# Strassen's method for three of eight pairs of k-tiles in w_up and the gates

## The chip, the cores and the metric

One core of a Trainium2 chip runs the whole program. The metric is the device time of one execution in microseconds (us), lower is better. The engines are TensorE (PE; PEld is its weight load), VectorE (DVE), ScalarE (ACT), GpSimd (POOL) and SyncE (SP, which issues the loads here).

## What is computed

Two layers of an encoder on 256 tokens of width 2048, all in float32:

```
proj  = x @ w_in            -> q/k/v of attention A and B, gate_A, gate_B (2048 columns each)
merged = sigmoid(gate_A) * (A @ w_pa) + sigmoid(gate_B) * (B @ w_pb)
x = LayerNorm(alpha * x + merged @ w_out)
gate, up = split(x @ w_up)                    # w_up: 2048 x 11264
x = LayerNorm(alpha * x + (silu(gate) * up) @ w_down)   # w_down: 5632 x 2048
```

## The kernel before

**Three matmuls for one product.** Each float32 operand is split into a high part (rounded to fp32r by a ScalarE copy) and a low part (VectorE: value minus high part). A product of two k-tiles is high x high + high x low + low x high: three matmuls into the same PSUM bank (`rows_product`, L215 to L217).

**Pieces.** Every weight matrix goes through a list of pieces of 512 KB (128 partitions x 1024 values: two k-tiles of 512 columns, or four of 256). `load_to` issues a piece's load on SP into one of N_RAW raw buffers, `split_to` makes `hi` and `lo` (L128, L129) in two of the N_UNITS unit buffers of 4 KB per partition, and `mm` runs its matmuls. `run` walks the list in order: for piece m it first writes out the splits up to AHEAD_SPLIT pieces further on (more near a LayerNorm), then `pre`, the matmuls, `post`, and then one entry of `background`. Every engine's queue follows this order; semaphores do the rest.

**Products.** `gemm_a` has x as the stationary operand: per k-tile and half of the tokens (t = 0, 1) three matmuls of 512 columns (or 256). One `gemm_a` over 2048 rows of 512 columns is 8 pieces, 96 matmuls, and takes one of the two double banks `acc`. `gemm_w` has the weights stationary (512 and 256 columns alternate). `aux` has four single banks for transposes and attention.

**The stages of a layer.** v, q and k products with attention in the background; the gates (`gate(c)`: two `gemm_a` and sigmoid, c = 0 to 3), each followed by `merge(c)` (w_pa, w_pb, products with the gates, and `turn_block`, which transposes the result); w_out with residual and LayerNorm (`residual_gemm`, `ln_turned`); then for 11 blocks c the gate and up products of w_up, silu (L748), the gating product (L752) and `turn_block`; after blocks 0 to 5 and 6 to 10 `residual_gemm` with that part of w_down. The last 512 columns of a `residual_gemm` with LayerNorm behind it are two blocks of 256 (the second by halves of the tokens).

**Background.** `turn_block` (L402: four transposes for each half, then the split L290, L291), attention, and after each LayerNorm the `affine` steps (L436, L437: res times g plus b; `load_affine` issues the loads into `gb`) are entries of `background`, one taken per piece.

Of the kernel before, what the change touches and what calls it, by code (L numbers as in the profile page):

```python
# [10 lines left out]
F32 = mybir.dt.float32  # L11
# [5 lines left out]
P = 128  # L17
# [20 lines left out]

N_RAW = 6
N_UNITS = 37  # L40
AHEAD_LOAD = 5
AHEAD_SPLIT = 3
AHEAD_NORM = 5
EARLY = 3


# [30 lines left out]
def trunk(ctx: ExitStack, tc: tile.TileContext, x, rel_bias, w_in, sink, w_pa, w_pb, w_out,  # L77
# [28 lines left out]
    background = []  # L106
    state = {"load": 0, "split": 0}
    norms = []

    def piece(src, kk, cc, mm, pre=None, post=None):  # L110
        pieces.append(dict(src=src, kk=kk, cc=cc, mm=mm, pre=pre, post=post))
        return pieces[-1]

    def load_to(m):
        while state["load"] < min(m, len(pieces)):
            pc = pieces[state["load"]]
            pc["raw"] = work.tile([P, pc["kk"], pc["cc"]], F32, name="raw", tag="raw", bufs=N_RAW)
            nc.sync.dma_start(pc["raw"], pc["src"])
            state["load"] += 1

    def split_to(m):
        while state["split"] < min(m, len(pieces)):
            load_to(state["split"] + 1 + AHEAD_LOAD)
            pc = pieces[state["split"]]
            raw = pc["raw"]
            hi = unit([P, pc["kk"], pc["cc"]], F32R, "whi")
            lo = unit([P, pc["kk"], pc["cc"]], F32R, "wlo")
            nc.scalar.activation(hi, raw, AF.Copy)  # L128
            nc.vector.tensor_tensor(out=lo, in0=raw, in1=hi.bitcast(F32), op=ALU.subtract)  # L129
            pc["hi"], pc["lo"] = hi, lo  # L130
            state["split"] += 1
# [118 lines left out]
    def gemm_a_halves(w, k0, k1, c0, width, xs, post, between):  # L250
# [21 lines left out]
        for j in range(k0, k1, kk):  # L272
            src = w[j * P:(j + kk) * P, c0:c0 + width].rearrange("(k p) c -> p k c", p=P)
            piece(src, kk, width, lambda pc, j=j: mm(j, pc))

    def lookup(tiles):
# [118 lines left out]
    def turn_block(src, tiles, name):  # L395

        def half(i):
# [5 lines left out]
            tiles.append(split_unit(ps, name))  # L403
        background.extend([lambda: None, lambda: half(0), lambda: half(1)])

# [243 lines left out]
    def layer(l, xt, pre, turn, after_last):  # L649
# [74 lines left out]
        def merge(c):  # L724
# [31 lines left out]
        after2, between2, ret = after_last(stats2)  # L756
        for half, (c0, c1) in enumerate(((0, 6), (6, 11))):
            for c in range(c0, c1):
                st = {}
                gemm_a(w_up[l], 0, KT, 512 * c, 512, x1s, lambda acc, st=st: post_gate(acc, st),  # L760
                       turn=(turn1 if c == 0 else None))
                gemm_a(w_up[l], 0, KT, D_FF + 512 * c, 512, x1s, lambda acc, st=st: post_up(acc, st))
            residual_gemm(w_down[l], 4 * c0, 4 * c1, lookup(hs), ALPHA if half == 0 else None,
                          None if half == 0 else stats2, after2, between2)
        if l < DEPTH - 1:
# [82 lines left out]
```

## Time and profile before

| what | value |
|---|---|
| median of 3 runs | 2767.43 us (2766.91 to 2768.36) |
| profiled execution | 2767.28 us, span 2765.5 us |
| TensorE busy | 2749.0 us, 99%, 13539 matmuls |
| VectorE busy | 1480.9 us, 54% |
| ScalarE busy | 1168.2 us, 42% |
| DMA | 531.8 MB, mean 192 GB/s |
| mean granted clock of TensorE | 0.998 of 2.4 GHz |

Busy times are sums of durations. Matmuls are pipelined, so a matmul's duration in a row is longer than its share of the time; the distance between the starts of two neighbours is what it costs. For VectorE and ScalarE too a following instruction that waits for nothing starts a little before the former one's end.

### The profile page before, as it was taken

The page shows a single profiled execution, that of the slowest core. Times are in us where ns is not written, and L with a number is a line of the kernel's source. Part 1 is how long each engine was busy: PE and PEld are TensorE (multiplying, and loading weights), DVE is VectorE, ACT ScalarE, POOL GpSimd, SP SyncE. Part 2 cuts the span into 40 slices and gives each one's busy share as a digit, 9 for nine tenths or more (in the row PEclk, how much of TensorE's full clock was granted, in tenths as well). Part 3 has the DMA queues.
Part 4 walks back from the last instruction along what each step waited for, and adds up shares of the span by engine and source line. Part 5 has one row for each costly group of instructions (what it writes and reads, how often), then busy time and mean ns, then how long its engine had stood idle before and what let it go on. Part 6 is the DMA issues. An engine that isn't in the chain of part 4 may idle for free.

```text
span 2765.5 us, 34763 instructions
## 1 busy us (share of the span) xinstructions
PE 2749.0 (99%) x13539; PEld 2319.5 (84%) x13539; DVE 1480.9 (54%) x1688; ACT 1168.2 (42%) x1407; POOL 5.4 (0%) x13
## 2 busy tenths in 40 slices
PE   9999999999999999999999999999999999999998
PEld 7888888888888888888889888888888888888887
DVE  5566554566644544445566655455665444444445
ACT  4454443444333443434344544433544344423441
POOL 0000000000000000000000000000000000000000
PEclk9999999999999999999999999999999999999999
DMA  8866665564655554655656666555645565555554
GB/s 255 241 183 181 185 202 178 187 229 149 225 184 183 208 204 158 211 177 191 215 162 201 179 183 191 177 201 179 232 162 198 183 205 205 183 183 183 187 209 145
DMA packets 359801, 531.84 MB, mean 192 GB/s; under 512 B 52288, under 2 KB 153664, under 8 KB 359636
## 3 DMA queue, kind: packets, MB, share of 16 engines
q1 hardware_dynamic: 358836, 528.31, 58.1%
q8 instruction: 106, 1.74, 0.3%
q10 hardware_dynamic: 800, 1.31, 0.1%
q14 instruction: 59, 0.48, 0.0%
HBM read 522.86 MB, written 6.68 MB: 191 GB/s over the span
## 4 chain that ended last, share of the span: by engine, by line
PE 98%; DVE 1%; DMA 0%; SPq 0%; issue 0%; ACT 0%; DVEq 0%; POOL 0%; ACTq 0%; POOLq 0%
PE acc L217 27%; PE acc L215 27%; PE acc L216 27%; PE acc L202 9%; PE acc L171 5%; PE aux L402 1%; PE aux L297 0%; PE aux L296 0%; PE aux L295 0%; DVE xT L392 0%; PE aux L562 0%; PE aux L528 0%; PE aux L620 0%; PE aux L544 0%; DMA res<-in_x_dram 0%; PE aux L370 0%
## 5 line engine op out<-in xcount | busy, mean ns | idle before, releaser
L129 DVE TENSOR_TENSOR wlo<-raw,whi 128x1024 fp32r<-128x1024 f32 x960 | 1127.4, 1221 | 474.5 <-ACT whi L128 455.4
L128 ACT ACTIVATE whi<-raw 128x1024 fp32r<-128x1024 f32 x960 | 971.5, 1054 | 434.9 <-DMA raw<-in_w_down_dram 142.1
L215 PE MATMUL acc<-whi,xT 128*128 128x512 f32 (+1 forms) x2176 | 848.7, 390 | 0.0
L217 PE MATMUL acc<-whi,xT 128*128 128x512 f32 (+1 forms) x2176 | 842.0, 387 | 0.0
L216 PE MATMUL acc<-wlo,xT 128*128 128x512 f32 (+1 forms) x2176 | 840.8, 386 | 0.0
L217 PEld LDWEIGHTS acc<-whi,xT 128*128 128x128 f32 x2176 | 409.1, 188 | 84.2
L215 PEld LDWEIGHTS acc<-whi,xT 128*128 128x128 f32 x2176 | 409.3, 188 | 80.8 <-issue 0.7
L216 PEld LDWEIGHTS acc<-wlo,xT 128*128 128x128 f32 x2176 | 409.4, 188 | 80.5
L202 PE MATMUL acc<-xT,whi 128*128 128x512 f32 x1088 | 387.0, 399 | 0.0
L171 PE MATMUL acc<-xT,wlo 128*128 128x256 f32 x1088 | 299.6, 280 | 0.0
L215 PE MATMUL acc<-whi,hT 128*128 128x512 f32 (+1 forms) x784 | 288.9, 368 | 0.0
L217 PE MATMUL acc<-whi,hT 128*128 128x512 f32 (+1 forms) x784 | 288.2, 368 | 0.0
L216 PE MATMUL acc<-wlo,hT 128*128 128x512 f32 (+1 forms) x784 | 288.0, 367 | 0.0
L202 PEld LDWEIGHTS acc<-xT,whi 128*128 128x128 f32 x1088 | 203.0, 188 | 43.3
L171 PEld LDWEIGHTS acc<-xT,wlo 128*128 128x128 f32 x1088 | 205.6, 189 | 2.6
L215 PEld LDWEIGHTS acc<-whi,hT 128*128 128x128 f32 x784 | 147.8, 189 | 24.3
L216 PEld LDWEIGHTS acc<-wlo,hT 128*128 128x128 f32 x784 | 147.9, 189 | 24.3
L217 PEld LDWEIGHTS acc<-whi,hT 128*128 128x128 f32 x784 | 147.8, 189 | 24.3
L290 ACT ACTIVATE hT<-aux 128x512 fp32r<-128x512 f32 x44 | 26.3, 598 | 315.2 <-PE aux L402 315.2
L752 DVE TENSOR_TENSOR sg<-sg,acc 128x1024 f32<-128x1024 f32 x22 | 26.9, 1221 | 202.3 <-PE acc L217 202.3
L215 PE MATMUL acc<-whi,mT 128*128 128x512 f32 (+1 forms) x320 | 111.5, 348 | 0.0
L217 PE MATMUL acc<-whi,mT 128*128 128x512 f32 (+1 forms) x320 | 111.0, 347 | 0.0
(133 smaller groups left out, 1503.8 us busy)
## 6 DMA issues: line engine op xcount, KB each, us to landing
raw<-in_w_up_dram SPq DMA_DIRECT2D x352, 512.0 KB, 4.7
raw<-in_w_in_dram SPq DMA_DIRECT2D x320, 512.0 KB, 4.9
raw<-in_w_down_dram SPq DMA_DIRECT2D x176, 512.0 KB, 5.5
raw<-in_w_out_dram SPq DMA_DIRECT2D x64, 512.0 KB, 5.6
raw<-in_w_pb_dram SPq DMA_DIRECT2D x32, 512.0 KB, 5.0
raw<-in_w_pa_dram SPq DMA_DIRECT2D x16, 512.0 KB, 5.9
bias<-ftab SPq DMA_DIRECT2D x96, 64.0 KB, 3.7
ftab<-fb SPq DMA_DIRECT2D x7, 640.0 KB
```

What stands on the lines that cost most here:

```text
L128: nc.scalar.activation(hi, raw, AF.Copy)
L129: nc.vector.tensor_tensor(out=lo, in0=raw, in1=hi.bitcast(F32), op=ALU.subtract)
L171: nc.tensor.matmul(st["acc"][:, n, 0:SEQ], lhsT=lo[:, k, n * P:(n + 1) * P], rhs=xs(4 * j + k)[:, 0, :], start=False, stop=False)
L202: nc.tensor.matmul(acc, lhsT=hi[:, k, n * P:(n + 1) * P], rhs=xs(kt).rearrange("p h t -> p (h t)"), start=first and not turn, stop=last)
L215: nc.tensor.matmul(o, lhsT=xk[:, 0, ts], rhs=hi, start=first, stop=False)
L216: nc.tensor.matmul(o, lhsT=xk[:, 0, ts], rhs=lo, start=False, stop=False)
L217: nc.tensor.matmul(o, lhsT=xk[:, 1, ts], rhs=hi, start=False, stop=last)
L290: nc.scalar.activation(hi, src, AF.Copy)
L402: nc.tensor.transpose(out=ps[:, k, t * P:(t + 1) * P], in_=src[:, t, c0:c0 + P], identity=ident)
L752: nc.vector.tensor_tensor(out=s, in0=s, in1=acc, op=ALU.mult)
```

## The change

`gemm_s` computes a block of 512 columns at c1 and one at c2 (gate_A and gate_B, or gate and up) together. Over a pair of k-tiles, the two token halves, two k-tiles and two column blocks are a 2 x 2 product of blocks; Strassen's form (Winograd's variant, 7 products) needs sums of x blocks, `sum_rows`, made once per layer and stage for the first SUMS = 3 pairs of k-tiles, and sums of weight blocks, made per block. PLAN = "SCSCSCCC": S is a pair of k-tiles with 7 products (four pieces, of which two have a load; VectorE adds t13 and t24 and splits them), C a pair with the usual 8 (two pieces). q1, q5, q6 and q7 take the four aux banks until `fold`, after the third S, brings them into two tiles e and f; q2, q3, q4 and x take both acc tiles, and the last C adds e and f. Pieces before the third S's end are `quiet`: no background is taken there. `turn_block` goes to a list `soon` that is taken before `background`.

It is used for gates c = 1 to 3 and w_up blocks c = 1 to 10, in both layers. w_down's parts follow blocks 0 to 3, 4 to 7 and 8 to 10 (three instead of two). Splits stand five pieces ahead instead of three; there are 7 raw buffers (6 before) and 36 units (37). In C steps 3, 5 and 6 of PLAN the low part of the left piece is made by ScalarE writing -raw and a DMA issued by GpSimd that adds raw to it; this is begun eight pieces ahead (its load eleven).

```diff
-N_RAW = 6
-N_UNITS = 37
+N_RAW = 7
+N_UNITS = 36
+SUMS = 3
+PLAN = "SCSCSCCC"
 AHEAD_LOAD = 5
-AHEAD_SPLIT = 3
+ADDED = (3, 5, 6)
+AHEAD_SPLIT = 5
+AHEAD_ADD = 8
+AHEAD_ADD_LOAD = 11
...
+    def add_to(m):
...
+        while state["add"] < min(m + AHEAD_ADD, len(pieces)):
+            pc = pieces[state["add"]]
+            if pc and pc.get("added"):
+                raw = pc["raw"]
+                pc["hi"], pc["lo"] = unit(list(raw.shape), F32R, "whi"), unit(list(raw.shape), F32R, "wlo")
+                nc.scalar.activation(pc["lo"], raw, AF.Copy, scale=-1.0)
+                nc.gpsimd.dma_start(pc["lo"], raw, accum_op=ALU.add)
+                nc.scalar.activation(pc["hi"], raw, AF.Copy)
+                pc["split"] = lambda pc: None
+            state["add"] += 1
...
+            add_to(m)
             split_to(m + 1 + ahead)
...
-            if background:
-                background.pop(0)()
+            if not pc.get("quiet") and (soon or background):
+                (soon or background).pop(0)()
...
+    def gemm_s(w, c1, c2, xs, sums, post, plan=PLAN):
+        names = {"S": ("q1", "q2", "q3", "q5", "q7", "q6", "q4"),
+                 "C": ("q2", "q2", "q4", "q4", "q3", "q3", "x", "x")}
...
+                st["even"], st["odd"] = acc_tile(), acc_tile()
+                st.update(q2=st["even"][:, 0, :], q3=st["even"][:, 1, :], q4=st["odd"][:, 0, :], x=st["odd"][:, 1, :])
...
+            def split2(pc):
+                raw = b["right"] = pc["raw"]
+                b["t13"] = unit([P, 2, 512], F32, "t13")
+                nc.vector.tensor_tensor(out=b["t13"][:, 0, :], in0=b["left"][:, 0, :], in1=raw[:, 0, :], op=ALU.add)
+                b["b22"] = unit([P, 2, 512], F32R, "b22")
+                split_into(b["b22"][:, 0, :], b["b22"][:, 1, :], raw[:, 1, :])
...
+            def split3(pc):
+                b["t24"] = unit([P, 2, 512], F32, "t24")
+                for o, x0, x1 in ((b["t13"][:, 1, :], b["right"][:, 0, :], b["right"][:, 1, :]),
+                                  (b["t24"][:, 0, :], b["t13"][:, 0, :], b["right"][:, 1, :])):
+                    nc.vector.tensor_tensor(out=o, in0=x0, in1=x1, op=ALU.add)
+                nc.vector.tensor_tensor(out=b["t24"][:, 1, :], in0=b["t24"][:, 0, :], in1=b["left"][:, 1, :], op=ALU.add)
+                b["h13"] = halves(b["t13"])
+            def split4(pc):
+                b["h24"] = halves(b["t24"])
+            def mm1(pc):
+                product("q1", rows(2 * p, 0), pc["hi"][:, 0, :], pc["lo"][:, 0, :])
+                product("q2", rows(2 * p + 1, 0), pc["hi"][:, 1, :], pc["lo"][:, 1, :])
...
+            def mm4(pc):
+                hi, lo = b["h24"]
+                product("q6", total(p, 2), hi[:, 0, :], lo[:, 0, :])
+                product("q4", rows(2 * p + 1, 1), hi[:, 1, :], lo[:, 1, :])
+                if last:
+                    fold()
...
+        def fold():
+            nc.scalar.activation(e[:, 0, :], st["q1"], AF.Copy)
+            nc.vector.tensor_tensor(out=d, in0=e[:, 0, :], in1=st["q6"], op=ALU.subtract)
+            nc.vector.tensor_tensor(out=e[:, 1, :], in0=d, in1=st["q7"], op=ALU.subtract)
+            nc.vector.scalar_tensor_tensor(f[:, 0, :], st["q5"], -1.0, d, op0=ALU.mult, op1=ALU.subtract)
+            nc.vector.scalar_tensor_tensor(f[:, 1, :], st["q5"], -1.0, e[:, 1, :], op0=ALU.mult, op1=ALU.subtract)
...
+            def block(pc, names_, extra):
...
+                for t, n in enumerate(names_):
+                    for k in range(2):
+                        product(n, rows(2 * p + k, t), pc["hi"][:, k, :], pc["lo"][:, k, :])
+                    if last:
+                        nc.vector.tensor_tensor(out=out_[:, t, :], in0=st[n], in1=st[extra][:, t, :], op=ALU.add)
...
         for c in range(4):
-            gate(c)
-            merge(c)
+            if c == 0:
+                gate(c)
+                merge(c)
...
+            else:
+                both(c)
+                merge(c)
...
-        for half, (c0, c1) in enumerate(((0, 6), (6, 11))):
+        chunks = ((0, 4), (4, 8), (8, 11))
+        for part, (c0, c1) in enumerate(chunks):
             for c in range(c0, c1):
                 st = {}
-                gemm_a(w_up[l], 0, KT, 512 * c, 512, x1s, lambda acc, st=st: post_gate(acc, st),
-                       turn=(turn1 if c == 0 else None))
+                if c > 0:
+                    gemm_s(w_up[l], 512 * c, D_FF + 512 * c, x1s, sums, post_both)
+                    continue
```

## Rows read from the trace of the kernel before

**Rows 1.** The page: busy us (share) x instructions, and the chain's shares.

```profile
PE 2749.0 (99%) x13539; PEld 2319.5 (84%) x13539; DVE 1480.9 (54%) x1688; ACT 1168.2 (42%) x1407; POOL 5.4 (0%) x13
...
PE 98%; DVE 1%; DMA 0%; SPq 0%; issue 0%; ACT 0%; DVEq 0%; POOL 0%; ACTq 0%; POOLq 0%
```

**Rows 2.** Timeline of PE in w_up: start us, us, engine, line, operation.

```profile
735.61 0.39 PE L215 MATMUL acc<-whi,xT 128*128 128x512 f32 x1
...
740.83 0.39 PE L217 MATMUL acc<-whi,xT 128*128 128x512 f32 x1
...
741.96 0.39 PE L216 MATMUL acc<-wlo,xT 128*128 128x512 f32 x1
```

**Rows 3.** Timeline of PE in w_out's 256-column block, first and last of 17.

```profile
639.74 0.28 PE L215 MATMUL acc<-whi,mT 128*128 128x256 f32 x1
...
641.66 0.28 PE L216 MATMUL acc<-wlo,mT 128*128 128x256 f32 x1
```

**Rows 4.** Timeline of PE around the transposes of half a block.

```profile
743.54 0.39 PE L217 MATMUL acc<-whi,xT 128*128 128x512 f32 x1
743.78 0.60 PE L402 MATMUL aux<-ident,sg 128*128 128x128 f32 x4
...
744.45 0.40 PE L216 MATMUL acc<-wlo,xT 128*128 128x512 f32 x1
```

**Rows 5.** The gating products of w_up's first part: ns min/median/max, first and last start.

```profile
L752 DVE TENSOR_TENSOR sg<-sg,acc x6: 1220/1220/1222, 696.8 to 919.2; 128x1024 f32<-128x1024 f32 x6
```

**Rows 6.** Window of those five periods: us, busy us (x) of each engine.

```profile
696.80:919.20 222.40, 222.40 (x1001) 184.06 (x1000) 110.88 (x103) 86.00 (x92) 0.00 (x0) 1.00 0.58 197
```

**Rows 7.** Timeline of DVE: neighbours at 692, a read of a product at 741.

```profile
692.08 0.69 DVE L437 TENSOR_TENSOR res<-res,gb 128x512 f32<-128x512 f32 x1
692.69 1.22 DVE L129 TENSOR_TENSOR wlo<-raw,whi 128x1024 fp32r<-128x1024 f32 x1
693.83 0.69 DVE L436 TENSOR_TENSOR res<-res,gb 128x512 f32<-128x512 f32 x1
694.55 0.69 DVE L437 TENSOR_TENSOR res<-res,gb 128x512 f32<-128x512 f32 x1
...
741.25 1.22 DVE L752 TENSOR_TENSOR sg<-sg,acc 128x1024 f32<-128x1024 f32 x1 [9.98 <-PE acc L217]
```

**Rows 8.** Groups of instructions by form: busy us, mean ns, idle before and releaser.

```profile
L129 DVE TENSOR_TENSOR wlo<-raw,whi 128x1024 fp32r<-128x1024 f32 x960 | 1127.4, 1221 | 474.5 <-ACT whi L128 455.4 <-PE acc L216 15.1
L128 ACT ACTIVATE whi<-raw 128x1024 fp32r<-128x1024 f32 x960 | 971.5, 1054 | 434.9 <-DMA raw<-in_w_down_dram 142.1 <-DMA raw<-in_w_up_dram 94.2 <-PE acc L217 66.3
```

**Rows 9.** Waits, SP's and the others': us in total, times, longest us.

```profile
SPq L118 <- DVE wlo L129: 2065.6, 884, 22.4
...
DVE wlo L129 <- ACT whi L128: 455.4, 249, 13.2
...
DVE res L436 <- DMA gb<-in_ln_g_dram: 19.1, 10, 3.3
```

**Rows 10.** DMA: share of 16 engines; issues with KB each and us to landing.

```profile
q1 hardware_dynamic: 358836, 528.31, 58.1%
...
raw<-in_w_up_dram SPq DMA_DIRECT2D x352, 512.0 KB, 4.7
...
gb<-in_ln_b_dram SPq DMA_DIRECT2D x16, 256.0 KB, 6.3
```

**Rows 11.** Timeline of ACT at the start: the seventh xT split.

```profile
27.04 0.59 ACT L290 ACTIVATE xT<-aux 128x512 fp32r<-128x512 f32 x1
```

**Rows 12.** Timeline of PE at the start, with idle time before.

```profile
9.17 0.30 PE L370 MATMUL aux<-ident,res 128*128 128x128 f32 x1 [2.29 <-DMA res<-in_x_dram]
10.46 0.52 PE L370 MATMUL aux<-ident,res 128*128 128x128 f32 x3 [0.98 <-DMA res<-in_x_dram]
...
11.08 0.63 PE L216 MATMUL acc<-wlo,xT 128*128 128x512 f32 x1
...
13.64 0.63 PE L216 MATMUL acc<-wlo,xT 128*128 128x512 f32 x1
```

More of the change, by code (lines that the diff above doesn't have):

```diff
@@ L106, in trunk @@
     background = []
-    state = {"load": 0, "split": 0}
+    soon = []
+    state = {"load": 0, "split": 0, "add": 0, "add_load": 0}
     norms = []
     def piece(src, kk, cc, mm, pre=None, post=None):
-        pieces.append(dict(src=src, kk=kk, cc=cc, mm=mm, pre=pre, post=post))
+        pieces.append(dict(src=src, kk=kk, cc=cc, mm=mm, pre=pre, post=post, split=split_plain))
         return pieces[-1]
@@ L116, in load_to, with split_plain, raw_tile @@
             pc = pieces[state["load"]]
-            pc["raw"] = work.tile([P, pc["kk"], pc["cc"]], F32, name="raw", tag="raw", bufs=N_RAW)
-            nc.sync.dma_start(pc["raw"], pc["src"])
+            if pc["src"] is not None and not pc.get("added"):
+                raw_tile(pc)
             state["load"] += 1
+    def split_plain(pc):
+        raw = pc["raw"]
+        pc["hi"] = unit(list(raw.shape), F32R, "whi")
+        pc["lo"] = unit(list(raw.shape), F32R, "wlo")
+        split_into(pc["hi"], pc["lo"], raw)
+    def raw_tile(pc):
+        pc["raw"] = work.tile([P, pc["kk"], pc["cc"]], F32, name="raw", tag="raw", bufs=N_RAW)
+        nc.sync.dma_start(pc["raw"], pc["src"])
+    def add_to(m):
+        while state["add_load"] < min(m + AHEAD_ADD_LOAD, len(pieces)):
+            pc = pieces[state["add_load"]]
+            if pc and pc.get("added"):
+                raw_tile(pc)
+            state["add_load"] += 1
+        while state["add"] < min(m + AHEAD_ADD, len(pieces)):
+            pc = pieces[state["add"]]
+            if pc and pc.get("added"):
+                raw = pc["raw"]
+                pc["hi"], pc["lo"] = unit(list(raw.shape), F32R, "whi"), unit(list(raw.shape), F32R, "wlo")
[4 more added lines that the diff above has]
+            state["add"] += 1
     def split_to(m):
@@ L124, in split_to @@
             pc = pieces[state["split"]]
[L125 to L130, printed above, removed]
+            pc["split"](pc)
             state["split"] += 1
@@ L403, in half @@
             tiles.append(split_unit(ps, name))
-        background.extend([lambda: None, lambda: half(0), lambda: half(1)])
+        soon.extend([lambda: None, lambda: half(0), lambda: half(1)])
     def ln_scale(stats, t):
@@ L756, in layer, with post_both @@
         after2, between2, ret = after_last(stats2)
-        for half, (c0, c1) in enumerate(((0, 6), (6, 11))):
+        sums = []
+        def post_both(gate_, up_):
+            nc.scalar.activation(gate_, gate_, AF.Silu)
+            nc.vector.tensor_tensor(out=gate_, in0=gate_, in1=up_, op=ALU.mult)
+            turn_block(gate_, hs, "hT")
+        chunks = ((0, 4), (4, 8), (8, 11))
+        for part, (c0, c1) in enumerate(chunks):
             for c in range(c0, c1):
                 st = {}
-                gemm_a(w_up[l], 0, KT, 512 * c, 512, x1s, lambda acc, st=st: post_gate(acc, st),
-                       turn=(turn1 if c == 0 else None))
+                if c > 0:
+                    gemm_s(w_up[l], 512 * c, D_FF + 512 * c, x1s, sums, post_both)
+                    continue
+                gemm_a(w_up[l], 0, KT, 512 * c, 512, x1s, lambda acc, st=st: post_gate(acc, st), turn=turn1)
                 gemm_a(w_up[l], 0, KT, D_FF + 512 * c, 512, x1s, lambda acc, st=st: post_up(acc, st))
-            residual_gemm(w_down[l], 4 * c0, 4 * c1, lookup(hs), ALPHA if half == 0 else None,
-                          None if half == 0 else stats2, after2, between2)
+                pieces[-12]["pre"] = lambda: background.__setitem__(slice(0, 0), [
+                    lambda i=i: sums.append(sum_rows(x1t[i])) for i in range(SUMS)])
+            last = part == len(chunks) - 1
+            residual_gemm(w_down[l], 4 * c0, 4 * c1, lookup(hs), ALPHA if part == 0 else None,
+                          stats2 if last else None, after2, between2)
         if l < DEPTH - 1:
```

87 lines of the change are left out of this document (added).

## The prediction

> **What bounds the kernel now.** I read the page's busy shares and its chain first [rows 1]: TensorE is busy 99% of the span and carries 98% of the chain that ended last, while VectorE is busy 54% and ScalarE 42%. A kernel in that state gets shorter by fewer or cheaper matmuls and by nothing else, as long as the other engines keep up. So the second reading is the price of one matmul. Its duration in the row (0.39 us) is pipelined and overlaps the next one; the price is the distance between starts. From the matmul that starts at 735.61 to the one at 741.96 there are 28 steps, 6.35 us, so 0.2268 us for a 512-column matmul [rows 2]. A 256-column matmul steps by 0.120 us (16 steps in 1.92 us), more than half of that [rows 3]. Turning one half block (four transposes) adds 0.46 us: from 743.54 to 744.45 two matmuls and the transposes take 0.91 us, and two matmuls alone take 0.45 [rows 4]. One pair of w_up products is now 192 x 0.2268 + 2 x 0.46 = 44.5 us, and from the first gating product of a layer to its sixth, five periods, it is 222.4 us, 44.48 each [rows 5], with TensorE busy for all of it [rows 6]. The account of TensorE therefore closes without any hidden idle time.
>
> The third reading is the slack beside it. In that stretch VectorE works 110.9 of 222.4 us and ScalarE 86.0 [rows 6]. VectorE's price is again the distance of starts: 1.14 us for a 1024-wide tensor_tensor, 0.61 us for a 512-wide one, 0.72 us where the next one needs its result [rows 7]. ScalarE's 1024-wide copy lasts 1.05 us [rows 8]. Result to reader is quick: a product's last matmul started at 740.83 and lasts 0.39; VectorE begins to read at 741.25 [rows 2, 7]. Loads run with slack: SP waits 2066 us in all for raw buffers to be freed by the subtraction [rows 9]; a 512 KB load then lands in 4.7 us [rows 10].
>
> **What the change removes.** A Strassen step needs 7 products of 3 matmuls where 8 were: 3 fewer. Three of the eight pairs of k-tiles get it, so 9 fewer of 192 per pair of column blocks. Per layer there are 3 such pairs among the gates and 10 in w_up, two layers: 26. 26 x 9 x 0.2268 = **53.1 us**. The chain carries all of it. The Trainium skill (TensorE: Matmul & The Clock Gate, Back-to-back issue gap) gives N / 2.4 + 2.5, 215.7 ns at 512 columns, by which 50.5 us would go and the result would come out 2.6 us later; the row's 226.8 ns decides.
>
> w_down in three parts instead of two leaves its matmuls as they are but shortens the part that ends in 256-column blocks from 20 to 12 k-tiles: 96 matmuls of 256 become 48 of 512 per layer, 96 x 0.120 - 48 x 0.2268 = 0.6 us, **1.3 us** in two layers. Its four extra updates of res per layer (1.22 us each on VectorE, as its 1024-wide subtraction [rows 8]) lie behind products of 16 us and more.
>
> **What it adds to VectorE and ScalarE.** VectorE, by the steps above: a Strassen pair needs three 1024-wide subtractions and five 512-wide operations, one of them behind its predecessor: 3 x 1.14 + 4 x 0.61 + 0.72 = 6.6 us. TensorE takes 21 x 0.2268 = 4.76 us for it, so **each Strassen pair costs VectorE more than TensorE**. A plain pair costs VectorE 2.28 and TensorE 5.44 us, and where the left low part goes by DMA only 1.14. The whole product: 3 x 6.6 + 7 x 1.14 + fold 2.7 + four adds 2.5 + the gating product 1.2 + two turned halves 1.4 = 35.6 us of VectorE beside 183 x 0.2268 + 0.92 = 42.4 us of TensorE, 84%. ScalarE: 22 copies of 1.05 at the most, six smaller ones of 0.6 [rows 11], silu no longer than a copy: 28 us or less. Neither is the bound on average, so the question is whether VectorE is ever late.
>
> I lay one period out, counted from its first matmul. TensorE: S1 0, C1 4.76, S2 10.2, C2 14.97, S3 20.4, C3 25.2, C4 31.5, C5 37.0, end 42.4 (the two turned halves lie in C3). Splits stand five pieces ahead in VectorE's order. The fold waits for q6 (24.7) and ends at 27.4; then C5's right split 28.5, a turned half (its transposes end at 28.35, ScalarE 0.6) 29.7, next S1's first split 30.8, the second turned half 32.8, S1's second to fourth splits 34.0, 37.1, 38.3. Now VectorE must wait for TensorE at the final adds: q2 39.1, q4 40.5, C1's left split 41.6, q3 42.2, x 43.3, gating product 44.5. The next period's q2 needs the bank freed by the add of q3, at 42.4 + 0.68 = 43.1: 0.9 us to spare. Going on: C1's right split 45.7, S2's four 46.8, 48.0, 51.1, 52.2. S2's third piece is wanted at 54.7: **3.5 us to spare, the smallest lead of a split**. If a split must wait for unit buffers of the piece just finished, S2's third can begin at 3.4 and S3's at 13.6, done by 6.5 and 16.7, wanted at 12.2 and 22.4. So no wait in a plain period.
>
> **Where I do expect waits.** The affine work of res stands in the background list, and background is popped only in pieces that are not quiet: for c = 1, 2, 3 of each layer two affine steps (2 x 1.33 us, from the 0.72 and 0.61 steps) fall between S1's third split and the add of q3. That add then ends at 43.9. The next Strassen product wants the bank at 43.1 (0.8 us late, twice per layer), and the w_down product after c = 3 wants it at 42.4 (1.5 us late): 3.1 per layer, **6.2 us**. If these steps wait for their gb load too (it lands in 6.3 us [rows 10], and affine waited 19.1 us in 10 places [rows 9]) up to 3 us more each, 18 in all; I take none, since in this order SP is waiting for raw buffers freed some 10 us earlier. The other ten places where a Strassen product gives way to a plain one have the bank free within 0.2 us: **2 us**. At the start, up to two more splits go ahead of the sixth to eighth xT split; ScalarE begins the seventh at 27.0 [rows 11], a little over one piece of 2.7 us before its use: between 0 and 2 x 1.14, I take **1.5 us**. The sums of xT (about 2.4 us of VectorE each, twelve) lie beside plain pieces where VectorE has 1.6 us of every 2.7 free, with five splits in hand. Cost nothing; without that cover 29 us.
>
> **The accumulating DMA.** No row shows one, nor a load issued by GpSimd. A plain 512 KB load takes 4.7 us [rows 10]; with two reads and a write for each value I bound it by 4.7 from below and by twice that, 9.4, from above, and take 7. The low part of C2's left half is issued when S1's third piece is done (3.4), after ScalarE's copy 4.5, and is wanted by the second matmul of that piece at 15.2: 10.7 us; C3's has 10.7, C4's 12.7. Inside the bounds it is hidden; the cover is these eight pieces. The Trainium skill (DMA: Bandwidth & Descriptors, Anatomy of one DMA) fits 2.0 us + bytes / 436e3 for a DMA from GpSimd, 3.2 us by estimate, by which the sum stays as it is; no run here shows it. The 78 transfers move 41 MB more beside 528 MB, on engines that are 58% taken now [rows 10].
>
> **Sum.** The profiled execution took 2767.28 us (span 2765.5, 0.15 us under the median of 2767.43): 2767.3 - 53.1 - 1.3 + 6.2 + 2 + 1.5 = 2722.6. VectorE's table has about 20 hand-overs per period that I priced at nothing; a tenth of a microsecond in half the periods brings me to **2724**.
>
> **Rivals.**
> - No wait at all (the table's affine waits vanish because VectorE runs further ahead): 2767.3 - 54.4 = 2713, up to 2719. For it: VectorE is at 84%. 0.18.
> - Forecast, 2719 to 2732. 0.50.
> - VectorE becomes the bound in places: each of 19 subtractions per period stands behind a ScalarE copy of 1.05 us or less, and that wait is VectorE's largest in this trace, 455 us in 249 places [rows 9]. If they cost 0.36 us each, VectorE needs the 42.4 us of TensorE, and 0.4 to 1.3 us of wait per period gives 10 to 34 us: 2732 to 2758. For it: a Strassen pair favours VectorE's lateness by 1.8 us. Against: ScalarE has 14 us free in a period. 0.20.
> - **Slower:** the accumulating DMA lands late. One wait of (landing - 10.7) per period, since the later ones are issued before it. It decides from 12.5 us on: 26 x 1.8 = 47 us eats the gain, the time is then above 2773; at 20 us it is about 2724 + 26 x 9.3 = 2966. A gap also brings the clock down: after idle of 2.29 and 0.98 us matmuls stepped by 0.427 us, the 1.2 GHz level, for 3 us [rows 12]. For it: the operation is unmeasured. Against: 12.5 is 2.7 times a load. The Trainium skill (SBUF — State Buffer, Who interferes with whom) says that GpSimd cannot write descriptors while VectorE runs in a two-port mode, and exempts tensor_tensor from that; VectorE's operations here are tensor_tensor, so by it this rival stays small. 0.09.
> - It doesn't do what it says (matmuls step slower between banks, say by 0.006 us): 2757 to 2773. Against: the plain loop already changes bank every three matmuls at 0.2268. 0.03.
>
> **Numbers.** The likeliest is 2724. From 2710 to 2756 the first three cases are in, all but some 0.13. Faster by over 0.2% (5.5 us, about what a measurement of this kernel tells from no change) 0.88, within 0.03, slower 0.09.
>
> **What will show it.** TensorE: 234 fewer matmuls of 512 columns, steps still 0.227, busy near 2700; period of w_up 42.4 us, longer by about 1 us for c = 1 and 2. VectorE busy for about 1481 + 26 x 16 + 39 = 1940 us (by durations: 4.7 more per Strassen pair, 5.5 for fold and adds, less 3.7 by DMA, then sums and updates). A wait of TensorE for the add of q3 in the first three Strassen products of w_up, none for low parts. GpSimd's DMA landing within 10 us. What would make it wrong: TensorE waiting for `lo` of the added pieces, or for t13 and t24 splits, in every period.

## The result, and the profile after

The changed kernel takes 2731.98 us (median of 4 runs, 2730.58 to 2733.23) beside 2767.17 us for the kernel before (4 runs, 2766.57 to 2768.36): a ratio of 0.9872, 95% interval 0.9855 to 0.9889. It is faster by 35 us, inside the range given and 8 us above the number given; 2731.98 lies at the very edge between the forecast's own band (2719 to 2732) and that of the rival in which VectorE is late in places. The profiled execution took 2733.02 us, with a span of 2731.2 us and a mean granted TensorE clock of 0.997.

The page of after, busy times and DMA: first the lines that answer to [rows 1], then queues and issues as in [rows 10].

```profile
PE 2701.2 (99%) x13209; PEld 2269.0 (83%) x13209; DVE 1894.5 (69%) x2354; ACT 1382.3 (51%) x1679; POOL 72.8 (3%) x91
...
q1 hardware_dynamic: 356788, 528.31, 58.9%
q0 software_dynamic: 11232, 40.90, 8.1%
...
raw<-in_w_up_dram SPq DMA_DIRECT2D x352, 512.0 KB, 5.2
...
wlo<-raw POOLq DMA_DIRECT2D x78, 512.0 KB, 6.9
```

TensorE lost 48 us of busy time and VectorE gained 414, and still TensorE is busy 99% of the span. The new queue q0 holds the 78 accumulating transfers, 41 MB, and lies beside loads that take 59% of the engines. Next, the gating products of w_up in a stretch without other work (name, count, ns min/median/max, first and last start), which answers to [rows 5]:

```profile
L955 DVE TENSOR_TENSOR sg<-sg x3: 1225/1226/1226, 1000.3 to 1085.2; 128x1024 f32<-128x1024 f32 x3
```

Two periods in 84.9 us: 42.45 each, where 44.48 were. What TensorE waits for most in after (what waited and for whom; us in total, times, longest):

```profile
PE aux L549 <- DMA res<-in_x_dram: 2.9, 2, 2.2
PE acc L329 <- DVE sg L414: 2.9, 5, 0.6
PE acc L329 <- DVE sg L908: 2.9, 2, 1.4
PE acc L245 <- DVE sg L414: 1.9, 2, 1.2
PE aux L330 <- DVE tlo L470: 1.6, 2, 0.8
```

L414 is the final add of a Strassen product, L908 the gating product of pa, L470 the low half of a split. Nowhere does TensorE wait for an accumulating DMA.

The chain of waits of after reaches back only into the last LayerNorm, so the account is made from steps: for each pair of neighbouring matmuls, the distance of their starts less the price of that form ([rows 2 to 4]), summed by place.

| term | forecast us | measured us |
|---|---|---|
| 234 fewer matmuls of 512 columns in 26 products | -53.1 | -53.1 |
| w_down: 192 fewer of 256 columns, 96 more of 512 | -1.3 | -1.3 |
| affine work of res, w_up c = 1 to 3, both layers | +6.2 | +5.9 |
| first Strassen product of the gates, both layers | 0 | +5.3 |
| start (first 44 to 46 us) | +1.5 | +2.7 |
| small steps of less than 0.15 us | +1.4 | +2.6 |
| other transitions | +2 | +1.0 |
| tail, from the last matmul's start to the end | 0 | +2.4 |
| sum; change of the span | -43.3 | -34.5; -34.3 |

The counts are exact: 10448 to 10310 matmuls of 512 columns, 2462 to 2270 of 256. All that is above the pace on TensorE (the steps' surplus over those prices, summed over the run) grew from 25.9 to 43.6 us, and the tail from 10.9 to 13.3.

**The gates' first Strassen product.** PE and DVE in after's timeline (start us, us, engine, line, operation, idle before and its releaser):

```profile
381.06 0.50 PE L329 MATMUL aux<-thi,sT 128*128 128x512 f32 x1
382.34 0.50 PE L330 MATMUL aux<-tlo,sT 128*128 128x512 f32 x1 [0.79 <-DVE tlo L470]
...
384.08 0.40 PE L331 MATMUL aux<-thi,sT 128*128 128x512 f32 x1
385.91 0.50 PE L329 MATMUL acc<-thi,xT 128*128 128x512 f32 x1 [1.43 <-DVE sg L908]
```

```profile
375.98 0.69 DVE L444 TENSOR_TENSOR v<-xT 128x512 f32<-128x512 f32 x1
...
378.53 0.69 DVE L470 TENSOR_TENSOR sT<-v,sT 128x512 fp32r<-128x512 f32 x1 [0.76 <-ACT sT L469]
...
381.07 2.51 DVE L470 TENSOR_TENSOR tlo<-t,thi 128x1024 fp32r<-128x1024 f32 x2
...
384.64 1.22 DVE L908 TENSOR_TENSOR sg<-sg,acc 128x1024 f32<-128x1024 f32 x1
```

The third sum of xT runs from 375.98 to 379.22, with a wait for ScalarE in it, just ahead of the splits of the first Strassen pair. So the first low half of a sum comes at 382.3, 1.06 us after the step that wanted it, and the merge product that empties a bank comes 1.60 us late: 2.66 us in each layer.

**The affine work.** There are seven such waits in the two layers, five like the one shown here and two of w_down behind c = 3. DVE and PE around the end of one product of w_up:

```profile
775.98 1.22 DVE L470 TENSOR_TENSOR tlo<-t,thi 128x1024 fp32r<-128x1024 f32 x1
777.11 0.68 DVE L615 TENSOR_TENSOR res<-res,gb 128x512 f32<-128x512 f32 x1
777.83 0.69 DVE L616 TENSOR_TENSOR res<-res,gb 128x512 f32<-128x512 f32 x1
778.44 1.22 DVE L470 TENSOR_TENSOR tlo<-t,thi 128x1024 fp32r<-128x1024 f32 x1
779.58 1.28 DVE L414 TENSOR_TENSOR sg<-acc,e 128x512 f32<-128x512 f32 x2
...
783.24 1.28 DVE L414 TENSOR_TENSOR sg<-acc,f 128x512 f32<-128x512 f32 x2
```

```profile
779.38 0.39 PE L331 MATMUL acc<-whi,xT 128*128 128x512 f32 x1
780.40 0.47 PE L329 MATMUL acc<-whi,xT 128*128 128x512 f32 x1 [0.63 <-DVE sg L414]
...
783.98 0.50 PE L329 MATMUL acc<-whi,xT 128*128 128x512 f32 x1
```

The matmul at 779.38 is the last of C5's left piece, so the one at 780.40 begins its right piece, q3. It starts 0.8 us late, just behind the first of the two adds at 779.58, that of q2. In a period without affine work that add stands where it is in time:

```profile
995.46 0.69 DVE L414 TENSOR_TENSOR sg<-acc,e 128x512 f32<-128x512 f32 x1
...
996.62 0.39 PE L329 MATMUL acc<-whi,xT 128*128 128x512 f32 x1
```

It ends at 996.15, 0.47 us before q3's first matmul at 996.62. One affine step of 1.33 us less 0.47 is 0.86; 0.8 was measured.

The wait that the prediction named stands right behind this one. VectorE works without a break from 775.98 to the add of q3, the first of the two in the row at 783.24; it ends at 783.92, and q2 of the next product begins at 783.98. Without the earlier wait TensorE would have asked for that bank at about 783.1 (an estimate: 783.98 less 0.8 and less the 0.07 us by which this step is late) and would have been held there for 0.8 us. So the earlier wait takes the place of the later one and does not come on top of it.

**The tail.** The last w_down part has 12 k-tiles instead of 20, and the second half of its tokens lasts 4.3 us on TensorE, while VectorE needs 6.6 us (2713.91 to 2720.52) for the LayerNorm of the first half:

```profile
2713.91 0.42 DVE L623 TENSOR_TENSOR res<-res,acc 128x256 f32<-128x256 f32 x1 [2.84 <-PE acc L247]
...
2717.91 0.28 PE L247 MATMUL acc<-whi,hT 128*128 128x256 f32 x1
...
2719.19 1.41 DVE L992 SCALAR_TENSOR_TENSOR res<-res,rstd,gb 128x512 f32<-128x512 f32 x2
2720.52 0.42 DVE L623 TENSOR_TENSOR res<-res,acc 128x256 f32<-128x256 f32 x1
```

The last matmul starts at 2717.91; its product is read only at 2720.52, when VectorE is done with the first half.

### The profile page after: what moved, and what is told of

Its sections match the earlier page's. It is cut to its first block, busy times and chain, and to the rows that moved or that the text cites. A ratio compares the mean times of both kernels' runs of the same rounds, so it can differ in the third digit from the quotient of the medians.

```text
span 2731.2 us, 35220 instructions
## 1 busy us (share of the span) xinstructions
PE 2701.2 (99%) x13209; PEld 2269.0 (83%) x13209; DVE 1894.5 (69%) x2354; ACT 1382.3 (51%) x1679; POOL 72.8 (3%) x91
## 5 line engine op out<-in xcount | busy, mean ns | idle before, releaser
L470 DVE TENSOR_TENSOR wlo<-raw,whi 128x1024 fp32r<-128x1024 f32 x804 | 951.2, 1220 | 199.0 <-ACT whi L469 155.3
L469 ACT ACTIVATE whi<-raw 128x1024 fp32r<-128x1024 f32 x804 | 815.4, 1052 | 275.3 <-PE acc L247 132.4
L329 PE MATMUL acc<-whi,xT 128*128 128x512 f32 x1118 | 440.3, 394 | 2.9 <-DVE sg L414 2.9
L331 PE MATMUL acc<-whi,xT 128*128 128x512 f32 x1118 | 435.9, 390 | 0.0
L330 PE MATMUL acc<-wlo,xT 128*128 128x512 f32 x1118 | 435.1, 389 | 0.0
L469 ACT ACTIVATE thi<-t 128x1024 fp32r<-128x1024 f32 x156 | 165.8, 1063 | 255.4 <-DVE t L367 234.5
L329 PEld LDWEIGHTS acc<-whi,xT 128*128 128x128 f32 x1118 | 209.9, 188 | 48.0 <-issue 4.8
L331 PEld LDWEIGHTS acc<-whi,xT 128*128 128x128 f32 x1118 | 209.8, 188 | 44.5
L330 PEld LDWEIGHTS acc<-wlo,xT 128*128 128x128 f32 x1118 | 210.2, 188 | 42.3
L232 PEld LDWEIGHTS acc<-xT,whi 128*128 128x128 f32 x1088 | 203.0, 188 | 43.3
L245 PE MATMUL acc<-whi,xT 128*128 128x512 f32 (+1 forms) x512 | 196.6, 384 | 0.3 <-ACT xT L469 0.3
L247 PE MATMUL acc<-whi,xT 128*128 128x512 f32 (+1 forms) x512 | 193.8, 379 | 0.6 <-DVE xT L470 0.6
L470 DVE TENSOR_TENSOR tlo<-t,thi 128x1024 fp32r<-128x1024 f32 x156 | 190.5, 1221 | 4.0 <-ACT thi L469 0.3
L246 PE MATMUL acc<-wlo,xT 128*128 128x512 f32 (+1 forms) x512 | 193.2, 377 | 0.0
```

The lines of the kernel that those rows point to most:

```text
L232: nc.tensor.matmul(acc, lhsT=hi[:, k, n * P:(n + 1) * P], rhs=xs(kt).rearrange("p h t -> p (h t)"), start=first and not turn, stop=last)
L245: nc.tensor.matmul(o, lhsT=xk[:, 0, ts], rhs=hi, start=first, stop=False)
L246: nc.tensor.matmul(o, lhsT=xk[:, 0, ts], rhs=lo, start=False, stop=False)
L247: nc.tensor.matmul(o, lhsT=xk[:, 1, ts], rhs=hi, start=False, stop=last)
L329: nc.tensor.matmul(o, lhsT=xk[0], rhs=hi, start=first, stop=False)
L330: nc.tensor.matmul(o, lhsT=xk[0], rhs=lo, start=False, stop=False)
```

## The experiments

Theory A: TensorE is the bound, and VectorE is late only where extra work is packed just ahead of a bank or a split that is wanted. Theory B: VectorE limits every Strassen product. Others are named in the expectations. All ratios are against the kernel before on the same chip, with 95% intervals; that kernel's medians beside the runs lie between 2766.74 and 2767.17 us, so that the times can be compared with each other too.

### The sums of xT moved ahead

```diff
-pieces[-6]["pre"] = lambda: (flush(), soon.extend([...]))
+for i in range(SUMS):
+    pieces[-18 + 4 * i]["pre"] = lambda i=i: xsums.append(sum_rows(xt[i]))
```

> The changed kernel with one edit: the three sums of xT for the gates are made in the second half of gate(0) instead of in the first three pieces of merge(0). Theory A (TensorE is the bound; VectorE is late only where extra work is packed into the pieces before a Strassen product): the two waits of TensorE in the first Strassen product of the gates (1.06 and 1.60 us at 381 and 384, the same at 1733 and 1736) go, 5.3 us in all: about 2726.5 us. Theory B (VectorE limits every Strassen product a little, the sums are one symptom): the waits move to a neighbouring product and the time stays within 1 us of 2732.

Measured: 2727.08 us (2726.5 to 2729.84), ratio 0.9858 (0.9843 to 0.9873). Both waits of the gates' first Strassen product are gone in both layers; a wait of 0.88 us per layer came up in the attention part before it. So the sums cost their place, not their length. At the two places 5.3 us of waits went and 1.8 came; the rest of the 4.9 us between the medians lies at the start, which this edit leaves alone and which differs from run to run (it is 2.2 us shorter in this profiled execution than in that of the changed kernel).

### The affine work, three times

First all of it in c = 0, with the four gb loads in front:

```diff
-background.extend([lambda: None] * 5)
-for c in range(4):
-    background.append(lambda c=c: load(c))
...
-        background.append(lambda c=c, t=t: affine(c, t, st[c]))
+        affine(c, t, st[c])
+background.extend([lambda c=c: load(c) for c in range(4)])
+background.extend([lambda c=c: both_halves(c) for c in range(4)])
```

> The changed kernel with one edit: after a LayerNorm the four gb loads come first in the background and each block's two affine steps in one entry, without the five empty entries, so that all of them lie in the plain products of block c = 0. Theory A: the waits of TensorE for the add of q3 at c = 1, 2 and 3 (0.8, 0.8 and 1.4 us in one layer, 0.8, 0.8, 0.5 and 0.8 in the other) go, 5.9 us: about 2726 us, and the periods of w_up at c = 1 and 2 fall from 43.4 to 42.45 us. Theory B: nothing or less than 2 us, because VectorE's work is the same.

Measured: 2738.3 us (2737.5 to 2739.84), ratio 0.9897 (0.9882 to 0.9912), a miss: slower than the changed kernel. The waits in c = 1 to 3 did go (period 42.45). But the lump now stood ahead of c = 1's first Strassen pair. PE there:

```profile
698.46 0.51 PE L330 MATMUL aux<-tlo,sT 128*128 128x512 f32 x1 [0.64 <-DVE tlo L470]
...
703.38 0.72 PE L329 MATMUL acc<-thi,xT 128*128 128x512 f32 x1 [4.19 <-DVE sg L947]
703.90 0.63 PE L330 MATMUL acc<-tlo,xT 128*128 128x512 f32 x1
704.33 0.63 PE L331 MATMUL acc<-thi,xT 128*128 128x512 f32 x1
```

It cost 0.64 and 4.19 us of idle time, and after the second the matmuls stepped by 0.43 us: the granted clock was 0.51 from 703.4 to 706.4, the 1.2 GHz level that [rows 12] showed behind the idle time at the start. Second try: the affine work and the loads of c = 1 to 3 in the first three pieces of the third Strassen pair, where VectorE has time before the fold.

```diff
+    calm = []
...
+            if pc.get("calm") and calm:
+                calm.pop(0)()
...
-                                   pre=None, post=None, quiet=True))
+                                   pre=None, post=None, quiet=True, calm=last and i < 3))
...
+                later = calm if c > 0 and vec % 4 == 0 else background
```

> The changed kernel with one edit: the affine steps (and gb loads) of blocks c = 1 to 3 are taken in the first three pieces of the third Strassen pair, where VectorE by the table waits 3.7 us for the fold anyway, instead of behind it. Theory A: the waits for the add of q3 in the first three Strassen products of w_up go and none comes: 5.9 us, about 2726 us, periods at c = 1 and 2 of 42.45 us. If the place is no better than plain block c = 0 of the former edit, waits appear there and the time is 2732 us or more.

Measured: 2734.02 us (2731.21 to 2737.4), ratio 0.9882 (0.9867 to 0.9897), a miss again. DVE in that stretch:

```profile
718.64 0.69 DVE L618 TENSOR_TENSOR res<-res,gb 128x512 f32<-128x512 f32 x1 [2.01 <-DMA gb<-in_ln_g_dram]
...
722.09 0.69 DVE L619 TENSOR_TENSOR res<-res,gb 128x512 f32<-128x512 f32 x1 [2.76 <-DMA gb<-in_ln_b_dram]
```

The load is issued so close ahead that VectorE stands for it, 17.8 us in six places for the first of the two loads alone, and all that is queued behind is late. Third try: the same places, with the four loads early in c = 0 (against the second try).

```diff
-            background.extend([lambda: None] * 5)
+            background.extend([lambda c=c: load(c) for c in range(4)])
+            background.extend([lambda: None] * 2)
...
-                later.append(lambda c=c: load(c))
```

> The former edit (affine steps of c = 1 to 3 in the third Strassen pair) with all four gb loads issued before, in block c = 0. In the former run VectorE stood 2.0 and 2.8 us at c = 1 for gb loads issued one short piece earlier; that ate the place it had free. Theory A: with the loads there in time the waits for the add of q3 in the first three Strassen products of w_up go, 5.9 us: about 2726 us, periods at c = 1 and 2 of 42.45 us. If waits stay, VectorE's free time before the fold is not there and theory A's table is wrong at that place: 2730 us or more.

Measured: 2725.05 us (2723.26 to 2726.02), ratio 0.9845 (0.9829 to 0.9862). DVE at the same place:

```profile
716.43 0.68 DVE L618 TENSOR_TENSOR res<-res,gb 128x512 f32<-128x512 f32 x1
...
722.69 0.68 DVE L403 TENSOR_TENSOR tmp<-e,aux 128x512 f32<-128x512 f32 x1
```

No wait is in front of the affine steps, the fold (L403) follows, all waits of TensorE for an add behind affine work are gone, and w_up's periods are 42.45 us for c = 1 to 3 too. So the same VectorE work costs 5.9 us, some 12 (the first try was 6.3 us slower than the changed kernel) or nothing, by its place, which is theory A.

### Splits three pieces ahead instead of five

```diff
-AHEAD_SPLIT = 5
+AHEAD_SPLIT = 3
```

> The changed kernel with splits three pieces ahead, as before the change. Theory A: by the table of one period, with three pieces the third and fourth split of the next product's first Strassen pair come behind the add of q4; the add of q3 ends 1.1 us after the bank is wanted and the fourth split 0.3 us late. 1.4 us in each of 26 periods: 36 us, about 2768 us, so nothing would be left of the gain. Theory C (the lead only covers loads, of which there are plenty): within 5 us of 2732.

Measured: 2765.99 us (10 runs, 2763.24 to 2770.58), ratio 0.9996 (0.9987 to 1.0006): without the lead nothing is left of the gain. Its PE waits:

```profile
PE acc L329 <- DVE sg L414: 20.0, 14, 2.4
PE aux L330 <- DVE tlo L470: 4.7, 4, 1.9
```

In the plain periods of w_up it is q2 of the next product that waits for the add of q3, 1.05 us each time, where 1.1 was expected. All above the pace is 78.0 us where the changed kernel has 43.6, and that 34.4 is the loss. VectorE's work is the same, 2354 instructions in both. A Strassen pair wants 6.6 us of VectorE in 4.76 us of TensorE; three pieces are not enough to have it done before.

### The accumulating DMA left out, and begun late

Left out, so that all low parts are VectorE's:

```diff
-ADDED = (3, 5, 6)
+ADDED = ()
```

> The changed kernel without the accumulating DMA: all low parts by VectorE's subtraction. VectorE has 3 x 1.14 us more per Strassen product, 39 of 42.4 us. Theory A: the table still closes (the last split before the fold is done at 24.6, the fold waits for 24.7), so 2732 us, at most 5 more, and VectorE's busy time rises by 95 us to 1990. Theory B: 1 us or more per period, 2758 us or above.

Measured: 2731.67 us (2731.1 to 2732.91), ratio 0.9873 (0.9858 to 0.9888), the same as the changed kernel, where theory B had 2758 us or above. The page:

```profile
PE 2701.3 (99%) x13209; PEld 2270.3 (83%) x13209; DVE 1979.2 (72%) x2432; ACT 1305.3 (48%) x1601; POOL 5.4 (0%) x13
```

The DMA takes 85 us from VectorE and gives none of it to the time. Then issued four pieces ahead instead of eight (the second line keeps `split_to`, which is five pieces ahead, from splitting these pieces on VectorE first):

```diff
-AHEAD_ADD = 8
+AHEAD_ADD = 4
...
+                    pieces[-2]["split"] = lambda pc: None
```

> The changed kernel with the accumulating DMA begun four pieces ahead instead of eight (its load still eleven ahead). In the changed kernel the low part lands 6.9, 6.1 and 6.7 us (medians for C2, C3 and C4) before its first matmul. Four pieces less are 8.2, 8.2 and 6.1 us. Theory A: TensorE waits 1.3 us at C2 and 2.1 us at C3 in each of 26 periods, up to 88 us: between 2780 and 2830 us; so the early start is what hides the DMA. Rival (the issue follows ScalarE's progress, which runs ahead of TensorE, and not the piece): no wait, 2732 us.

Measured: 2861.89 us (2859.1 to 2865.41), ratio 1.0344 (1.0329 to 1.036): the direction as expected, by more than expected. PE waits and one of them in the timeline:

```profile
PE acc L330 <- DMA wlo<-raw: 85.7, 37, 5.6
```

```profile
403.04 0.79 PE L330 MATMUL acc<-wlo,xT 128*128 128x512 f32 x1 [5.65 <-DMA wlo<-raw]
```

The landing itself rose, from 6.9 us (median of all) to 9.4 and 9.8 us for the second and third of a product. These two are now issued 2.8 us apart (median; 5.4 in the changed kernel), so that both are under way at once for most of the time; the first of a product, which is alone, lands in 7.0. And behind 18 of the 37 waits TensorE's steps went to 0.43 us, 131 such steps in all, some 26 us more (granted clock 0.985 over the span); behind the other 19 they did not. Both were missing in what was expected. So the rival of a late DMA is real, and the lead of eight pieces is its whole cover: in the changed kernel the low parts land 6.9, 6.1 and 6.7 us (medians; least 3.6) before the matmul that reads them.

### Number and order of the Strassen pairs

Two pairs instead of three:

```diff
-SUMS = 3
-PLAN = "SCSCSCCC"
+SUMS = 2
+PLAN = "SCSCCCCC"
```

> The changed kernel with two Strassen pairs per product instead of three (plan SCSCCCCC, two sums). Theory A: 3 x 0.2268 us more in each of 26 periods, 17.7 us, less up to 2 us for one sum fewer before the gates: 2748 to 2750 us. Theory B (VectorE limits, and it has 5 us less to do per period): clearly less than 17.7 us lost, 2735 to 2742 us.

Measured: 2740.78 us (2739.31 to 2742.33), ratio 0.9906 (0.9891 to 0.9921). That is in theory B's stretch and not in A's. But what it rests on is not B's: 78 matmuls more cost their 17.7 us in full, and what is above the pace fell from 43.6 to 32.0 us, 7.8 of these 11.6 at the gates' first product (1.08 us per layer instead of 2.66) and beside the affine work (one wait of 0.61 per layer, where the changed kernel has 5.9 us in both); the rest is at the start and in small steps, half each. A had left these waits as they were. This run alone doesn't decide; the runs with the waits moved away do.

Three pairs, without plain pairs between them:

```diff
-PLAN = "SCSCSCCC"
+PLAN = "SSSCCCCC"
```

> The changed kernel with the three Strassen pairs one behind the other (plan SSSCCCCC); the work is the same, its order not. Theory A: a Strassen pair takes 6.6 us of VectorE and 4.76 of TensorE, and only the plain pairs between give that back; by the table S3's third piece is ready 13.0 us after the period's start and wanted at 11.6: 1.4 us in each of 26 periods, 36 us, about 2768 us. Rival (the order does not matter while VectorE has 16% free): 2732 us.

Measured: 2818.77 us (2818.06 to 2823.11), ratio 1.0192 (1.0175 to 1.0209): the direction as expected, the size far over. PE waits:

```profile
PE aux L581 <- ACT e L399: 35.8, 22, 1.9
PE aux L330 <- DVE tlo L470: 21.4, 29, 0.8
```

The second is the splits that come late, as expected. The first is a wait that was in no table: the transposes (L581) want an aux bank, and these are held by products until the fold's first copy (L399). It starts at 1002.72 here and the transposes at 1003.35, held for 1.61 us; in the changed kernel the copy starts at 978.16 and the transposes at 984.77. So, as these two traces show it, the plain pairs between do two things: they give VectorE time, and they put the fold ahead of the transposes.

### The tail, and all together

Last part of w_down with 16 k-tiles instead of 12:

```diff
-        chunks = ((0, 4), (4, 8), (8, 11))
+        chunks = ((0, 4), (4, 7), (7, 11))
```

> The changed kernel with w_down's parts behind blocks 0 to 3, 4 to 6 and 7 to 10: the last part has 16 k-tiles instead of 12. Theory A: 0.6 us more of TensorE (256-column blocks grow by a third), but the last token half then runs 5.8 instead of 4.3 us, so that VectorE's work on the first half of the final LayerNorm is nearer to its end when the last matmul is: last matmul's start to the end falls from 13.3 to about 11.9 us. Together 1 us less, about 2731 us. Rival (the longer end has another cause, such as the output's DMAs): the end stays 13.3 us.

Measured: the tail is 11.88 us instead of 13.33, as expected. In the time, 2731.79 us (2731.37 to 2733.06), ratio 0.9872 (0.9858 to 0.9887), it can't be told: executions of one kernel lie further apart than the 1 us that was expected (2730.58 to 2733.23 for the changed one).

The sums moved ahead, the affine work in calm pieces with its loads early, this split of w_down, and three splits ahead in the first 12 pieces:

```diff
-            ahead = min(AHEAD_SPLIT, 1 + m)
+            ahead = min(AHEAD_SPLIT if m >= 12 else 3, 1 + m)
```

> Sums in gate(0), affine steps in the third Strassen pair with early loads, 16 k-tiles in w_down's last part, and three splits ahead for the first twelve pieces. Theory A adds the parts: 2732 - 4.9 (measured) - 5.9 - 1.0 - 1.2 = 2719 us. If the parts overlap or new waits appear, 2722 to 2727.

Measured: 2717.85 us (2717.26 to 2721.8), ratio 0.9824 (0.981 to 0.9839). This beats both kernels: 49 us below the kernel before, 14 below the changed one. Of the four edits the last was not run by itself. The page and the largest wait of PE:

```profile
PE 2697.5 (99%) x13257; PEld 2271.9 (84%) x13257; DVE 1893.8 (70%) x2354; ACT 1381.8 (51%) x1679; POOL 73.0 (3%) x91
```

```profile
PE aux L552 <- DMA res<-in_x_dram: 2.4, 2, 1.6
```

VectorE is as busy as in the changed kernel (1893.8 and 1894.5 us), and no wait of more than 0.25 us is left in any Strassen product. Against this kernel, a fourth Strassen pair:

```diff
-SUMS = 3
-PLAN = "SCSCSCCC"
+SUMS = 4
+PLAN = "SCSCSCSC"
-ADDED = (3, 5, 6)
+ADDED = (3, 5, 7)
```

> The former kernel with four Strassen pairs (plan SCSCSCSC, four sums). TensorE has 17.7 us less; VectorE by the table 39.9 of 41.8 us per period. Theory A: what counts is the order at the end of a product, where with one plain pair left behind the fold the add of q3 ends 0.1 to 0.5 us after the bank is wanted: 2719 - 17.7 + 26 x 0.1 to 0.5, 2704 to 2715 us. Theory B (above some 85% VectorE is the bound): no gain or a loss, 2719 us or more.

Measured: 2732.78 us (2731.34 to 2736.84), ratio 0.9878 (0.9863 to 0.9892). That is 15 us slower than the kernel that it starts from, in theory B's stretch; A had 2704 to 2715, so A's sum missed. The matmuls shrink by their 17.7 us, and 33 us of waits come in: in most periods TensorE is held up by 0.82 or 1.36 us, up to 2.64 beside affine work, where A had 0.1 to 0.5. PE and DVE at the end of one product:

```profile
PE acc L332 <- DVE sg L417: 26.0, 26, 2.5
```

```profile
991.78 0.50 PE L332 MATMUL acc<-whi,xT 128*128 128x512 f32 x1 [0.67 <-DVE sg L417]
```

```profile
987.38 0.69 DVE L403 TENSOR_TENSOR tmp<-e,aux 128x512 f32<-128x512 f32 x1 [2.72 <-PE aux L334]
...
989.91 1.22 DVE L473 TENSOR_TENSOR tlo<-t,thi 128x1024 fp32r<-128x1024 f32 x1
991.04 1.28 DVE L417 TENSOR_TENSOR sg<-acc,e 128x512 f32<-128x512 f32 x2
```

VectorE idles 2.72 us before the fold, as it must wait for the last Strassen products. Then fold, split and add stand in a row, with one plain pair of TensorE beside them, and the add comes too late for the bank: the matmul at 991.78 is the first of q3, and it begins as the first add of the row at 991.04, that of q2, ends. These are the same two banks that met beside the affine work in the changed kernel.

Whether VectorE's share is the limit can be read in single periods, from one gating product to the next (us, busy us (x) of PE, PEld, DVE, ACT, POOL, clock, DMA share, GB/s): first in this run, then in the run without the accumulating DMA.

```profile
995.63:1038.40 42.77, 41.57 (x186) 34.10 (x185) 37.16 (x44) 27.89 (x31) 2.59 (x3) 1.00 0.87 264
```

```profile
1000.50:1042.95 42.45, 42.45 (x193) 35.15 (x192) 39.08 (x45) 23.00 (x27) 0.00 (x0) 1.00 0.59 198
```

VectorE is busy for 87% of the first, in which TensorE waits, and for 92% of the second, in which it does not. So B's limit of some 85% is not there. What decides is the order at the end of the product, as A has it, but A's table looked at the add of q3 and the next product's q2, and the wait came earlier, at q3 for the add of q2.

## Why the prediction was right, and where its steps were off

- **What bounds it, and the price of a matmul.** Right. 2 x 42.45 us measured for two plain periods against 42.4; the steps stayed at 0.227 when banks alternate, 234 matmuls fewer gave 53.1, and w_down 1.3. "It doesn't do what it says" is out. The 215.7 ns that the Trainium skill gives for the gap of an isolated matmul (TensorE: Matmul & The Clock Gate, Back-to-back issue gap) would make the period's 183 matmuls 2.0 us shorter than the trace does; the row decides.
- **No wait in a plain period, with five splits ahead.** Right, and the lead carries it: with three ahead the ratio was 0.9996. The table's 35.6 us of VectorE for a period were 35.75 in the one from 1000.30 to 1042.75. VectorE's total came to 1894.5 us, not 1940: I added durations to a busy time, and a busy time is not the sum of durations, as the section on the profile before has it, but counts once the 0.08 us or so by which neighbours overlap ([rows 7]: 1.22 long, 1.14 apart). All its durations add up to 1556.2 us before and 2004.8 after; those grew by 449 us where I had 459.
- **The affine waits.** The size was right, 5.9 us for 6.2, and moving the work brought it back (the third try). The place was wrong for five of the seven waits: I had the next Strassen product waiting for the add of q3, with 0.9 us to spare. It was the right piece of the same pair, q3, waiting for the add of q2 in the other half of the same accumulator tile, with 0.47 us to spare. The bank wait of w_down after c = 3 was where I had it (1.38 and 0.83 us for 1.5). The step at fault is "The next period's q2 needs the bank freed by the add of q3": it left out a reader of the same tile that comes earlier. But the wait that it named was there behind the other, 0.8 us as well, so that the right size is not luck.
- **"The sums of xT cost nothing".** Wrong, the largest miss: 5.3 us. The cover that I named, free VectorE time and five splits in hand, is true on average. But the third sum stood in VectorE's order just ahead of the first Strassen splits, and those five splits in hand are plain pieces; what waits behind the sum is a Strassen pair, of which each costs VectorE 1.8 us more than TensorE.
- **The tail.** A missing term, +2.4 us: I counted the shorter last part as cheaper columns and did not ask what hides the LayerNorm of the first tokens. 16 k-tiles gave 1.45 us of it back.
- **Start and hand-overs.** The start cost 2.7 us more where I had 1.5, but it differs by some 2 us between runs of the same start. Small steps and other transitions came to 3.6 us together, where I had 3.4.
- **The accumulating DMA.** Hidden, as forecast, q0's engines beside 59% of loads. That it landed in 6.9 us where I took 7 is luck: 7 was the middle between two bounds, 4.7 and 9.4. The Trainium skill's fit (DMA: Bandwidth & Descriptors, Anatomy of one DMA) gave 3.2 us by estimate; the trace shows 6.9, more than twice that, and the sum is the same by either. That it is worth nothing (left out: 2731.67) was in the table, where VectorE has 6.8 us to spare per period, but I did not draw it out.
- **The rivals.** The forecast and "VectorE late in places" both hold a part: the waits are of the second kind, without its mechanism (the copies of ScalarE ahead of subtractions: VectorE's wait for them fell from 455 us to 155 [rows 9]). The slower rival needs the late issue to become true. Not all of VectorE's operations are tensor_tensor, as that rival has it: two of the four of a fold (L402, L403) are scalar_tensor_tensor; the DMA landed in time all the same.

**Left open.** Why q3 waits for q2's add, beside the affine work and with four Strassen pairs in every period, was read off the code (both halves of one accumulator tile) and the trace and not tried apart. Nor was it tried apart whether two accumulating DMAs under way at once are what made them land later. The 2.6 us of small steps were not followed one by one, nor why the start's waits for transfers differ between runs.

## What to carry to other kernels

When one engine carries 98% of the chain, price its instructions by the distance of their starts, and the gain of having fewer comes out to the tenth of a microsecond; what is left to find out is lateness. For that, a helper engine's share says little (92% of a period without a wait in one run, 87% with one in another): lay out its order for one period, look at what stands just ahead of each bank and split that is wanted, and give every lump of other work a place there, with its loads long before. A transfer that takes work from an engine with time to spare gains nothing and can lose much.

## What the runs showed of the hardware

- An accumulating 512 KB DMA within the chip, issued by GpSimd (0.86 us busy each), landed in 6.9 us in the median, between 4.5 and 8.0, beside loads at 59% of the DMA engines. Where two were issued closer together, they took more (medians): 6.8 and 7.0 us at a distance of 5.4, both 8.4 at 3.8 (three Strassen pairs in a row, where TensorE waits for none of them), 9.4 and 9.8 at 2.8 (the late issue). The view of its line in after:

```profile
L150 POOL DMA_DIRECT2D wlo<-raw x78: 859/859/1017, 387.0 to 2626.0; - x78
```

- The loads of w_up landed in 5.2 us (median) beside it, in 4.7 before and in 4.7 in the changed kernel without it.
- Behind an idle stretch of 4.19 us in full flow TensorE stepped by 0.43 us (granted clock 0.51); behind waits of 0.63 us it did not (the steps behind the one at 780.40 are 0.23 to 0.31). In the run with the late DMA, 18 waits between 1.80 and 5.65 us were followed by such steps and 19 between 0.30 and 3.05 us were not, so that the length of one wait did not tell.
